# A mask product in bfloat16 instead of float32 in a hybrid decoder block

## The chip, the cores and the metric

The kernel runs on one core of a Trainium2 chip. The metric is the time of one execution on the device in microseconds (us); lower is better. The core has four engines that matter here: TensorE (PE in the profile) multiplies matrices, VectorE (DVE) and ScalarE (ACT) work on elements, GpSimd (POOL) issues the gathers of expert rows. SyncE (SP) issues most of the other transfers. TensorE's weight loads have a row of their own, PEld.

## The reference, cut to what matters

One decoder layer over 1024 tokens of width 1024. Three mixers run on the same normalised input and are merged by gates; an expert layer follows, in which every token takes 16 of 16,384 experts in each of 8 heads. The change touches the first mixer, stick-breaking attention with 8 heads of 64:

```python
def block(args):
    q_blk, n = args
    z = jnp.einsum('bhqd,bhkd->bhqk', q_blk, k).astype(jnp.float32) * scale
    qpos = n * Q_BLOCK + jnp.arange(Q_BLOCK)
    past = kpos[None, :] < qpos[:, None]
    log_keep = jnp.where(past, jax.nn.log_sigmoid(-z), 0.0)
    between = lax.cumsum(log_keep, axis=3, reverse=True) - log_keep
    a = jnp.where(past, jnp.exp(jax.nn.log_sigmoid(z) + between), 0.0)
    return jnp.einsum('bhqk,bhkd->bhqd', a.astype(v.dtype), v)
```

A query sees only keys before its own position. Blocks of 128 keys wholly in the past need no mask; a block on the diagonal does.

## The kernel before, in words

**Tiles and groups.** The 1024 tokens are eight tiles of 128, taken in three groups of 2, 3 and 3 tiles (`GROUPS`). Each group goes through `phase1`: normalisation, projections, stick attention, dilated attention, attention to the memory tokens, gating, output projection and the choice of experts. Tiles 4 and 6 (`DENSE`) later go through all experts in `dense`; the other six fetch their chosen expert rows.

**Stick attention.** `stick_breaking` (line 419) works on four pairs of heads, and in each pair on sub-groups of two tiles (`stick_part`, line 499) or one (`stick_single`, line 450). For every block of 128 keys, from the diagonal back, the scores of both heads go into one PSUM bank `z`. In a diagonal block a second product adds the mask to the scores: the identity `ident` as one operand, the table `diagneg` as the other, -1e30 where a key isn't in the past (lines 463 and 513). ScalarE then takes Abs, Exp and Ln, VectorE forms `sp`, and later products with `ntri` (line 151) add the sums over keys to the same bank before the last Exp. A helper, `Pipe`, issues the second and third part of a block one and two pieces later, so that TensorE has other products in between. A group of 2 tiles has 2 diagonal tiles, a group of 3 has 3; with four pairs and two heads there are 8 tiles x 4 x 2 = 64 mask products. The tables are made once, near the start, on VectorE (lines 147 to 151).

**Products.** Nearly all products go through `mm` (line 112), which issues one and adds its estimated time to a ledger, `cost[0]`. Its rule for a product of n columns and 128 rows is `4 * (n / 2.4 + 2.5)`; a transpose books 120 (`flip`, line 120).

**Expert steps.** `Experts.step` (line 1133) handles four tokens at a time for one of four positions: POOL gathers 128 rows of `u` and 128 rows of `v` (line 1097), 4 KB each; VectorE multiplies and sums (line 1151); after four steps ScalarE takes Gelu, VectorE spreads the weights, and TensorE adds up the rows of `v` (line 1177, eight products a step as the profile counts them). The token's own row is spread over partitions by bfloat16 products with the table `which` (line 1090). There are 768 steps.

**The order.** The program is written out in one order for each engine. A planner at the end of the kernel (lines 1409 to 1446) mixes expert steps with pieces of `phase1` and `dense`. It keeps two clocks. A piece adds its booked cost times `SLOW` (1.38 in phase 1, 1.1 in the dense stage) to `pe`, and its loaded bytes over `BW` (295, then 360) to `dma`. A step adds `TOKEN_NS` = 700 to `pe` and `TOKEN_BYTES` over `BW` to `dma`:

```python
due = max(due + LEAST, pe - LEAST)
while filler[0] is not None and (dma > pe or pe < due):
    a, b = fill(1)
    pe += a
    dma += b
pe += TOKEN_NS
dma += TOKEN_BYTES / bw[0]
if ex.step():
    done += 1
```

So before each step the planner issues mixer or dense pieces until the TensorE clock has reached the DMA clock. When the pieces are used up, the remaining steps run alone. Before the first group has chosen its experts there are no steps to mix in.

Of the kernel before, what the change touches and what calls it, by code (L numbers as in the profile page):

```python
# [7 lines left out]
F32 = mybir.dt.float32  # L8
BF = mybir.dt.bfloat16
# [3 lines left out]
OP = mybir.AluOpType  # L13
# [64 lines left out]
def block_kernel(ctx: ExitStack, tc: tile.TileContext, io):  # L78
    nc = tc.nc
# [16 lines left out]
    const = pool("const", 1)  # L96
# [8 lines left out]
    cost = [0.0]  # L105
# [3 lines left out]
    def bank():  # L109
        return ps.tile([128, 512], F32, name="bank")  # L110

    def mm(out, lhsT, rhs, **kw):
        n = 1
        for d in rhs.shape[1:]:
            n *= d
        cost[0] += 4 * (n / 2.4 + 2.5) * out.shape[0] / 128
        nc.tensor.matmul(out, lhsT, rhs, **kw)  # L117
# [5 lines left out]
    def actf(out, in_, f, **kw):  # L123
        s = SETS.get(f)
        if s and table[0] != s:
            nc.scalar.preload_act_table_set(s)  # L126
            table[0] = s
        nc.scalar.activation(out, in_, f, **kw)  # L128
# [4 lines left out]
    dmat = tmp.tile([128, 2, NS], F32, name="S", bufs=1)[:, 0, :128]  # L133
# [11 lines left out]
    nc.vector.tensor_scalar(dmat, dmat, rows[:, 2:3], None, op0=OP.subtract)  # L145
    ident = keep.tile([128, 128], F32, bufs=1)
    nc.vector.tensor_scalar(ident, dmat, 0.0, None, op0=OP.is_equal)
    diagneg = const.tile([128, 128], F32)
    nc.vector.tensor_scalar(diagneg, dmat, 0.0, -HUGE, op0=OP.is_le, op1=OP.mult)
    ntri = const.tile([128, 128], F32)  # L150
    nc.vector.tensor_scalar(ntri, dmat, 0.0, -1.0, op0=OP.is_le, op1=OP.mult)
# [267 lines left out]
    def stick_breaking(pipe, weights, hT, n0, G, oT):  # L419
        N = G * 128  # L420
        t0 = n0 * 128
        for p in range(4):
# [23 lines left out]
            for i, g in subs(G):  # L446
                args = pipe, kT, v, q[:, :, i * 128:(i + g) * 128], n0 + i, oT[:, p, i * 128:(i + g) * 128]
                yield from stick_single(*args) if g == 1 else stick_part(*args[:5], g, args[5])

    def stick_single(pipe, kT, v, q, n, out):  # L450

        S = tmp.tile([128, 2, NS], F32, name="S", bufs=1)[:, :, :128]
        box = {}
        for b in range(n, -1, -2):
            bs = [b, b - 1][:b + 1]
            m = len(bs)
            z = bank().rearrange("p (x s n) -> p x s n", x=2, s=2)
            for x, y in enumerate(bs):
                for s in range(2):
                    mm(z[:, x, s], kT[:, y * 128:(y + 1) * 128], q[:, s], start=x == 0 and s == 0, stop=False,  # L460
                       skip_group_check=True)
                    if y == n:
                        mm(z[:, x, s], ident, diagneg, start=False, stop=False, skip_group_check=True)
            e = tmp.tile([128, EW], F32, name="e")[:, :512].rearrange("p (x s n) -> p x s n", x=2, s=2)
            actf(e[:, :m], z[:, :m], AF.Abs)
            actf(e[:, :m], e[:, :m], AF.Exp, scale=-1.0)
            actf(e[:, :m], e[:, :m], AF.Ln, bias=1.0)
            sp = tmp.tile([128, 2, NS], F32, name="sp").rearrange("p x (s n) -> p x s n", s=2)
            nc.vector.scalar_tensor_tensor(sp[:, :m], z[:, :m], 0.0, e[:, :m], op0=OP.max, op1=OP.add)

            def part1(b=b, m=m, z=z, e=e, sp=sp):
                for x in range(m):
                    mm(z[:, x], ntri, sp[:, x], start=False, stop=False, skip_group_check=True)
                    if b < n:
                        mm(z[:, x], nones, S, start=False, stop=False, skip_group_check=True)
                if m == 2:
                    mm(z[:, 1], nones, sp[:, 0], start=False, stop=True, skip_group_check=True)
                actf(e[:, :m], z[:, :m], AF.Exp)
                if b >= 2:
                    if b == n:  # L480
                        nc.vector.tensor_add(S, sp[:, 0], sp[:, 1])
                    else:
                        for x in range(m):
                            nc.vector.tensor_add(S, S, sp[:, x])

            def part2(b=b, bs=bs, e=e):
                if b == n:
                    box["o"] = bank()
                for x, y in enumerate(bs):
                    for s in range(2):  # L490
                        mm(box["o"][64 * s:64 * s + 64, :128], v[:, y, 64 * s:64 * s + 64], e[:, x, s],
                           start=y == n, stop=y == 0, skip_group_check=True)
                if bs[-1] == 0:
                    nc.vector.tensor_copy(out, box["o"][:, :128])
            pipe.tick()
            pipe.push(part1, part2)
            yield

    def stick_part(pipe, kT, v, q, n0, G, out):
        N = G * 128  # L500
        nl = n0 + G - 1
        S = tmp.tile([128, 2, NS], F32, name="S", bufs=1)
        box = {}
        for b in range(nl, -1, -1):
            dg = b >= n0
            c0 = (b - n0) * 128 if dg else 0
            off = c0 + 128 if dg else 0
            z = bank().rearrange("p (s n) -> p s n", s=2)
            for s in range(2):
                mm(z[:, s, c0:N], kT[:, b * 128:(b + 1) * 128], q[:, s, c0:N],  # L510
                   start=s == 0, stop=False, skip_group_check=True)
                if dg:
                    mm(z[:, s, c0:c0 + 128], ident, diagneg, start=False, stop=False,
                       skip_group_check=True)
            e = tmp.tile([128, EW], F32, name="e")[:, :2 * NS].rearrange("p (s n) -> p s n", s=2)
            actf(e[:, :, c0:N], z[:, :, c0:N], AF.Abs)
            actf(e[:, :, c0:N], e[:, :, c0:N], AF.Exp, scale=-1.0)
            actf(e[:, :, c0:N], e[:, :, c0:N], AF.Ln, bias=1.0)
            sp = tmp.tile([128, 2, NS], F32, name="sp")
            nc.vector.scalar_tensor_tensor(sp[:, :, c0:N], z[:, :, c0:N], 0.0, e[:, :, c0:N],  # L520
                                           op0=OP.max, op1=OP.add)

            def part1(b=b, c0=c0, off=off, dg=dg, z=z, e=e, sp=sp):
                for s in range(2):
                    mm(z[:, s, c0:N], ntri, sp[:, s, c0:N], start=False, stop=False,
                       skip_group_check=True)
                    if off < N:
                        mm(z[:, s, off:N], nones, S[:, s, off:N], start=False, stop=s == 1,
                           skip_group_check=True)
                actf(e[:, :, c0:N], z[:, :, c0:N], AF.Exp)  # L530
                if b:
                    if dg:
                        nc.vector.tensor_copy(S[:, :, c0:off], sp[:, :, c0:off])
                    if off < N:
                        nc.vector.tensor_add(S[:, :, off:N], S[:, :, off:N], sp[:, :, off:N])

            def part2(b=b, c0=c0, e=e):
                if b == nl:
                    box["o"] = bank()
                for s in range(2):  # L540
                    mm(box["o"][64 * s:64 * s + 64, c0:N], v[:, b, 64 * s:64 * s + 64],
                       e[:, s, c0:N], start=b == nl, stop=b == 0, skip_group_check=True)
                if b == 0:
                    nc.vector.tensor_copy(out, box["o"][:, :N])
            pipe.tick()
            pipe.push(part1, part2)
            yield
# [949 lines left out]
```

## Time and profile before

| | |
|---|---|
| median of 3 runs | 3574.66 us (3574.15 to 3581.68) |
| profiled execution | 3564.13 us, span 3562.4 us |
| mean granted TensorE clock | 0.936 |
| TensorE busy | 3189.3 us, 90% |
| GpSimd busy (gathers) | 1768.1 us, 50% |
| bytes moved by DMA | 1185.56 MB, 333 GB/s |
| of these, gathered expert rows | 805.40 MB |

The profile is one execution; its time lies below the three timed runs. A busy TensorE is not TensorE at its peak, since the length of a product in the profile contains its latency and products overlap. The distance between the starts of two products tells what each takes.

### The profile page before, as it was taken

Reading aid. Unit: us, or ns where it says so; the run is one execution under the profiler, and the core shown is the slowest. Engines: PE = TensorE matmul, PEld = TensorE weight load, DVE = VectorE, ACT = ScalarE, POOL = GpSimd, SP = SyncE. Lnnn points to the kernel's source line nnn. Section 1 sums busy time; section 2 is a strip of 40 time slices with the busy share of each in tenths; the row PEclk is TensorE's granted clock in tenths of the full one; section 3 lists DMA queues with packets and bytes.
Section 4 is the critical chain, followed back from the end, with each engine's and each line's share of the span. In section 5 each row is a group of like instructions: output and inputs, shape, how many; then the busy total and the mean of one; then the engine's idle time right before and its main releaser. Section 6 shows DMA issues by size and latency. Waiting matters only on the chain.

```text
span 3562.4 us, 61070 instructions
## 1 busy us (share of the span) xinstructions
PE 3189.3 (90%) x22930; PEld 2359.5 (66%) x22930; DVE 2356.0 (66%) x6003; ACT 1371.6 (39%) x2747; POOL 1768.1 (50%) x1544
## 2 busy tenths in 40 slices
PE   6999879989999889999998999776779999999954
PEld 6889856656555766666565657654558888888720
DVE  5444597565644469995656665788867677777654
ACT  4443345554411214656544221322224444444410
POOL 0000036655566565766555655566645444544476
PEclk9989989999999999999999999887899999999965
DMA  4425659999899999989998999998999999999999
GB/s 151 140 84 182 221 210 342 336 342 340 318 405 392 403 361 348 331 329 356 328 351 292 391 386 401 350 326 338 399 384 391 365 382 382 390 383 373 349 380 377
DMA packets 346431, 1185.56 MB, mean 333 GB/s; under 512 B 38744, under 2 KB 80216, under 8 KB 326680
## 3 DMA queue, kind: packets, MB, share of 16 engines
q0 software_dynamic: 221184, 805.40, 59.6%
q1 hardware_dynamic: 102672, 337.95, 25.9%
q10 hardware_dynamic: 22280, 38.31, 2.8%
q8 instruction: 181, 2.97, 0.3%
q14 instruction: 114, 0.93, 0.1%
HBM read 1142.18 MB, written 39.32 MB: 332 GB/s over the span
## 4 chain that ended last, share of the span: by engine, by line
PE 60%; DVE 14%; DMA 14%; issue 5%; ACT 4%; POOL 2%; ACTq 0%; SPq 0%; POOLq 0%; DVEq 0%
PE bank L117 30%; PE bank L1195 21%; DMA u<-in_u,iT 7%; PE po L1177 7%; DVE u L1151 4%; DMA v<-in_v,iT 2%; PE pb L1090 2%; DMA b3d<-sp 1%; PE bank L121 1%; POOL u L1097 1%; POOL v L1097 1%; ACT L126 1%; DMA g<-gd 1%; ACT e L128 1%; DMA gd<-g 1%
## 5 line engine op out<-in xcount | busy, mean ns | idle before, releaser
L1097 POOL DMA_INDIRECT u<-in_u,iT x768 | 920.9, 1199 | 965.0 <-DVE i L865 487.7
L1097 POOL DMA_INDIRECT v<-in_v,iT x768 | 846.4, 1102 | 817.8 <-PE po L1177 644.5
L1151 DVE SCALAR_TENSOR_TENSOR u<-u,hb 128x1024 f32<-128x1024 f32 x768 | 927.0, 1223 | 437.6 <-ACT hb L128 274.3
L1177 PE MATMUL po<-v,wz 128*32 128x256 f32 x6144 | 443.7, 416 | 150.2 <-DMA v<-in_v,iT 83.2
L117 PE MATMUL bank<-wide,w 128*128 128x384 f32 x1536 | 520.8, 493 | 2.6 <-DMA w<-in_w_gate 2.6
L117 PEld LDWEIGHTS bank<-wide,w 128*128 128x128 f32 x1536 | 293.1, 193 | 202.7 <-issue 11.2
L1177 PEld LDWEIGHTS po<-v,wz 128*32 128x32 f32 x6144 | 181.8, 115 | 369.6 <-DMA v<-in_v,iT 115.7
L128 ACT ACTIVATE hb<-pb 128x512 f32<-128x512 f32 x384 | 208.2, 595 | 400.0 <-PE pb L1090 257.3
L117 PEld LDWEIGHTS bank<-w,wide 128*128 128x128 f32 x2304 | 263.0, 192 | 7.5 <-issue 2.3
L117 PE MATMUL bank<-w,wide 128*128 128x128 f32 x2304 | 265.3, 275 | 0.2 <-DMA w<-in_w_out 0.2
L1195 PE MATMUL bank<-hh,ul 128*128 128x256 f32 x848 | 240.0, 283 | 1.3 <-DVE ul L1275 1.3
L1195 PE MATMUL bank<-hh,uh 128*128 128x256 f32 x848 | 240.9, 284 | 0.0
L1195 PE MATMUL bank<-hl,uh 128*128 128x256 f32 x848 | 239.9, 283 | 0.0
L128 ACT ACTIVATE e<-bank 128x512 f32<-128x512 f32 (+2 forms) x208 | 109.6, 527 | 277.4 <-PE bank L117 249.3
L1195 PE MATMUL bank<-vh,wh 128*128 128x512 f32 x512 | 203.0, 403 | 2.2 <-ACT vh L128 2.2
L1195 PE MATMUL bank<-vl,wh 128*128 128x512 f32 x512 | 201.8, 394 | 2.4 <-DVE vl L1275 2.3
L1195 PE MATMUL bank<-vh,wl 128*128 128x512 f32 x512 | 199.5, 390 | 0.0
L126 ACT ACT_TABLE_LOAD x144 | 184.8, 1283 | 20.6 <-issue 8.4
L128 ACT ACTIVATE w<-bank 128x256 f32<-128x256 f32 x128 | 49.3, 385 | 366.0 <-PE bank L1195 285.1
L1275 DVE TENSOR_TENSOR vl<-vr,vh 128x1024 fp32r<-128x1024 f32 x128 | 157.1, 1227 | 31.8 <-ACT vh L128 31.8
L117 PE MATMUL bank<-big,w 128*128 128x128 f32 (+1 forms) x1024 | 175.9, 330 | 0.6 <-DMA w<-in_w_pq 0.6
L1195 PE MATMUL bank<-u 128*128 128x256 f32 x544 | 164.9, 303 | 10.2 <-ACT u L128 10.2
(297 smaller groups left out, 5887.9 us busy)
## 6 DMA issues: line engine op xcount, KB each, us to landing
ur<-in_uT SPq DMA_DIRECT2D x64, 1024.0 KB
vr<-in_vd SPq DMA_DIRECT2D x64, 1024.0 KB
w<-in_w_in SPq DMA_DIRECT2D x102, 512.0 KB
w<-in_w_gate SPq DMA_DIRECT2D x72, 512.0 KB
w<-in_w_pq SPq DMA_DIRECT2D x48, 512.0 KB
g<-gd SPq DMA_DIRECT2D x16, 1024.0 KB
w<-in_w_o SPq DMA_DIRECT2D x48, 256.0 KB
w<-in_w_out SPq DMA_DIRECT2D x24, 512.0 KB
```

Of the source, the lines that this page charges most:

```text
L117: nc.tensor.matmul(out, lhsT, rhs, **kw)
L121: nc.tensor.transpose(out, in_, ident)
L126: nc.scalar.preload_act_table_set(s)
L128: nc.scalar.activation(out, in_, f, **kw)
L1090: nc.tensor.matmul(pb, which[:, jj].rearrange("p q s -> p (q s)"), box["b3"][:, f], start=True, stop=True)
L1097: nc.gpsimd.indirect_dma_start(out=t, out_offset=None, in_=io[kind], in_offset=bass.IndirectOffsetOnAxis(ap=ap, axis=0))
L1151: nc.vector.scalar_tensor_tensor(u, u, 1.0, self.hb, op0=OP.mult, op1=OP.mult, accum_out=self.parts[:, i:i + 1])
L1177: nc.tensor.matmul(po[32 * k:32 * k + 32, h:h + 256], wz[:, i, :], v[:, 256 * k:256 * k + 256], start=jj == 0 and i == 0, stop=jj == QB - ...
L1195: nc.tensor.matmul(out, lhsT, rhs, **kw)
L1275: nc.vector.tensor_sub(lo, r[:, x], hi)
```

## The change

The mask product moves from `mm` into a function of its own. Its operands become bfloat16: a second identity table, `eye`, and `diagneg` in bfloat16. The function books 60 in the ledger where `mm` booked 4 x (128 / 2.4 + 2.5) = 223. Both calling places, in `stick_single` and `stick_part`, use it. The identity table `ident` stays float32 for its other users.

```diff
     nc.vector.tensor_scalar(ident, dmat, 0.0, None, op0=OP.is_equal)
-    diagneg = const.tile([128, 128], F32)
+    eye = const.tile([128, 128], BF)
+    nc.vector.tensor_scalar(eye, dmat, 0.0, None, op0=OP.is_equal)
+    diagneg = const.tile([128, 128], BF)
     nc.vector.tensor_scalar(diagneg, dmat, 0.0, -HUGE, op0=OP.is_le, op1=OP.mult)
...
+    def mask(z):
+
+        cost[0] += 60
+        nc.tensor.matmul(z, eye, diagneg, start=False, stop=False, skip_group_check=True)
+
     def stick_single(pipe, kT, v, q, n, out):
...
                     if y == n:
-                        mm(z[:, x, s], ident, diagneg, start=False, stop=False, skip_group_check=True)
+                        mask(z[:, x, s])
...
                 if dg:
-                    mm(z[:, s, c0:c0 + 128], ident, diagneg, start=False, stop=False,
-                       skip_group_check=True)
+                    mask(z[:, s, c0:c0 + 128])
```

## The prediction

> **What bounds the kernel now.** I read the page first, for the balance of the engines and the chain that ended last.
>
> ```profile
> span 3562.4 us, 61070 instructions
> ...
> PE 3189.3 (90%) x22930; PEld 2359.5 (66%) x22930; DVE 2356.0 (66%) x6003; ACT 1371.6 (39%) x2747; POOL 1768.1 (50%) x1544
> ...
> DMA  4425659999899999989998999998999999999999
> ...
> PE bank L117 30%; PE bank L1195 21%; DMA u<-in_u,iT 7%; PE po L1177 7%; DVE u L1151 4%; DMA v<-in_v,iT 2%; PE pb L1090 2%; DMA b3d<-sp 1%; PE bank L121 1%; POOL u L1097 1%; POOL v L1097 1%; ACT L126 1%; DMA g<-gd 1%; ACT e L128 1%; DMA gd<-g 1%
> ```
>
> TensorE is busy for 90% of the span and the chain of waits runs mostly through its products, but from the seventh slice on the DMA engines are also nearly full. So I cut the span into stages: start, stick attention of the first group, rest of that group, the first long stretch in which expert steps run between the pieces of the mixer, the second one, the dense experts, and the end, where only expert steps are left. Columns: time, busy time and instruction count of each engine, granted clock, DMA share, GB/s.
>
> ```profile
> 77.00:134.00 57.00, 57.00 (x456) 53.27 (x455) 19.26 (x29) 26.81 (x49) 0.00 (x0) 1.00 0.50 158
> 134.00:488.00 354.00, 314.89 (x2510) 289.19 (x2510) 200.88 (x540) 139.11 (x294) 0.00 (x0) 0.92 0.47 149
> 488.00:1590.00 1102.00, 1025.60 (x7248) 693.74 (x7247) 740.63 (x2124) 454.65 (x860) 674.39 (x602) 0.97 0.95 355
> 1590.00:2443.00 853.00, 757.56 (x5500) 517.30 (x5498) 568.80 (x1579) 300.73 (x686) 494.70 (x442) 0.93 0.93 348
> ...
> 2650.00:3400.00 750.00, 744.10 (x5316) 630.75 (x5316) 534.91 (x829) 346.12 (x574) 359.53 (x277) 1.00 0.98 376
> 3400.00:3562.00 162.00, 77.53 (x542) 16.04 (x540) 82.06 (x156) 17.66 (x46) 116.06 (x115) 0.55 0.99 389
> ```
>
> The first gather of the expert steps is where I set the third border:
>
> ```profile
> L1097 POOL DMA_INDIRECT u<-in_u,iT x768: 932/940/3240, 488.3 to 3544.1; - x192
> ```
>
> Until 488 us TensorE alone is the limit (57.00 of 57.00 us busy in the first stick stage, DMA half idle). From 488 to 3400 us TensorE and DMA are both near full. In the last 162 us DMA is at 0.99 while TensorE is half idle. Each expert step has two gathers on POOL, so 115 of them are 57.5 steps, or 162 / 57.5 = 2.82 us a step.
>
> Next, the products that change: count, duration and place.
>
> ```profile
> L117 PEld LDWEIGHTS bank<-diagneg,ident x128: 187/192/192, 79.9 to 1642.1; 128*128 128x128 f32 x128
> L117 PE MATMUL bank<-diagneg,ident x128: 271/275/275, 80.0 to 1642.2; 128*128 128x128 f32 x128
> L149 DVE TENSOR_SCALAR diagneg<-S x1: 217/217/217, 6.0 to 6.0; 128x128 f32<-128x128 f32 x1
> ```
>
> ```profile
> 77.00:134.00 57.00, 6.17 (x32) 5.47 (x32) 0.00 (x0) 1.00 0.50 158
> ...
> 488.00:1590.00 1102.00, 16.20 (x84) 13.89 (x84) 0.00 (x0) 0.97 0.95 355
> 1590.00:2443.00 853.00, 2.31 (x12) 1.97 (x12) 0.00 (x0) 0.93 0.93 348
> ```
>
> A float32 product appears as two instructions, so 128 are 64 mask products: 16 in the first group, 48 in the other two, all before 1643 us. Their 275 ns is a latency; what one takes from TensorE is the distance between starts, which the timeline of the first stick block shows (start, length, instruction):
>
> ```profile
> 80.33 0.30 PEld L117 LDWEIGHTS bank<-diagneg,ident 128*128 128x128 f32 x2
> ...
> 80.44 0.39 PE L117 MATMUL bank<-diagneg,ident 128*128 128x128 f32 x2
> ...
> 80.55 0.30 PEld L117 LDWEIGHTS bank<-qpad,big 128*128 128x128 f32 x2
> 80.66 0.60 PE L117 MATMUL bank<-qpad,big 128*128 128x256 f32 x2
> ```
>
> The mask starts at 80.44 and the product behind it at 80.66: 0.22 us for a mask, 0.11 for each half. A weight load starts when the product ahead of it starts, not earlier (the load at 80.55 goes with the mask's second half, which began 0.11 after 80.44), and its own product follows 0.11 later.
>
> **The change part by part.** *The product.* The bfloat16 mask is one instruction with one load, where the float32 mask is two and two. No row shows a 128x128 bfloat16 product; the nearest are the row-spreading products and the loads of other widths:
>
> ```profile
> L1090 PEld LDWEIGHTS <-which x384: 95/98/207, 459.3 to 3522.4; 96*128 96x128 bf16 x192
> L1090 PE MATMUL pb<-b,which x384: 376/381/634, 459.4 to 3522.8; 96*128 96x512 bf16 x192
> ```
>
> ```profile
> 506.53 0.60 PE L1090 MATMUL pb<-b,which 96*128 96x512 bf16 x2
> ```
>
> ```profile
> L117 PEld LDWEIGHTS bank<-ident,s x160: 106/113/158, 485.8 to 2408.4; 128*32 128x32 f32 x160
> ...
> L117 PEld LDWEIGHTS bank<-e,big x416: 132/136/232, 85.4 to 1674.5; 128*64 128x64 f32 x139
> ```
>
> Two bfloat16 products of 512 columns take 0.60 us with 0.38 for the last, so 0.22 between starts; a quarter of the columns is 0.055. That is the lower bound of a mask's price. The bfloat16 load is short (98 ns against 192), so the mask's own weights are ready in time. But float32 loads grow with the columns (113, 136, 192 ns for 32, 64, 128), and the load behind the mask is nearly always a float32 one of 128 columns, which can start only with the mask's product and takes its 0.11: the next product starts 0.11 after the mask, however short that was. This is the upper bound, and my value, since the four lines of the timeline show exactly this succession. Saved per mask: 0.11 us (at most 0.165). The Trainium skill ("TensorE: Matmul & The Clock Gate", Back-to-back issue gap) gives 55.6 ns for a lone 128-column bfloat16 product and about 81 ns in a stream of load and product pairs. With these the sum below would be about -3.7 and -2.7 us. No run here shows either.
>
> *First group, 77 to 134 us.* TensorE has no gap there, and the chain of waits runs through it without a break:
>
> ```profile
> 112.64 2.03 PE bank L1195 x17
> 114.68 1.87 PE bank L117 x12
> 116.55 2.87 PE bank L1195 x24
> 119.42 6.55 PE bank L117 x52
> ```
>
> So 16 x 0.11 = 1.8 us go off the path (at most 16 x 0.165 = 2.6), and all behind starts earlier by as much.
>
> *The ledger.* The diff also replaces the charge that the order planner books for a mask. A product of 128 columns costs 4 x (128/2.4 + 2.5) = 223 in `mm`; `mask` books 60. Times SLOW = 1.38 that is 225 ns less per mask, and 48 x 0.225 = 10.8 us less over groups two and three (in the first no expert step is being balanced). The planner runs mixer pieces until its TensorE clock has caught up with its DMA clock. A step adds TOKEN_BYTES / 295 = 1,073,152 / 295 = 3638 ns to one and 700 to the other, a gap of 2938 ns; with 10.8 us less booked, 10.8 / 2.94 = 3.7 fewer steps stand between the mixer pieces, and 3.7 more are left at the end. Moved with each step are two gathers on POOL's queue, the multiply on DVE, its eight products and a share of the row spreading. Dense pieces keep their own ratio of steps.
>
> *Stretch from 488 us.* If TensorE is the limit there, it gets shorter by 48 x 0.11 = 5.3 us and by the moved steps' products:
>
> ```profile
> 1317.60 3.64 PE po L1177 x32
> ```
>
> Eight of these are 3.64 / 32 x 8 = 0.91 us a step, and half a spreading product is 0.11: 3.7 x 1.02 = 3.8, together 9.1 us (7.9 + 3.8 = 11.7 with the cheaper mask). If DMA is the limit, 3.7 x 1.073 MB at the 355 GB/s of the stage = 11.2 us, and the cheaper mask adds nothing. TensorE at 93% and DMA at 0.95 do not decide it; I take the middle of 9.1 and 11.2, 10.1.
>
> *The end.* 3.7 more steps at 2.82 us: +10.4 us. The chain there is gathers, so nothing hides them:
>
> ```profile
> 3428.50 8.46 DMA u<-in_u,iT
> 3436.98 1.25 DVE u L1151 x2
> 3439.32 7.88 DMA u<-in_u,iT
> ```
>
> *The tables.* `eye` is one more DVE instruction near 6 us, about 0.2 us like the one quoted for `diagneg`. The first product waits for this:
>
> ```profile
> 11.93 0.72 ACT L128 ACTIVATE sq<-big 128x256 f32<-128x256 f32 x2 [9.47 <-DMA big<-in_memT]
> ```
>
> The load of the memory tokens hides it; without that cover it would cost its 0.2 us. Storage is unchanged (two tables of 256 bytes a partition for one of 512).
>
> **Sum.** -1.8 - 10.1 + 10.4 = -1.5 us, with ends -2.6 - 11.7 + 10.4 = -3.9 and -1.8 - 9.1 + 10.4 = -0.5. The profiled execution itself took 3564.13 us (span 3562.4 and 1.7 around it), so it would take 3562.6. It lies 10.5 under the median of the runs, 3574.66, which moves to 3573.2. About 0.2%, 7 us, is what a measurement can tell from no change: I forecast none that can be told.
>
> **Rivals.**
>
> *Faster: the new order closes gaps.* From 488 to 1590 us TensorE is idle 76 us and DMA 5%, 55 us, because steps and mixer pieces wait for each other. ScalarE is among the causes: it swaps its function table whenever a step's Gelu falls between Exp and Ln of an attention block.
>
> ```profile
> 488.00:1590.00 1102.00, 115.47 (x90) 0.97 0.95 355
> ```
>
> 90 swaps of 1.28 us (rows of line 126 alone). Fewer steps there mean fewer swaps: 3.7 steps are about one group of four, at most two swaps, 2.6 us; the rest would have to come from a better fit of the order, a tenth of the gaps, 5 to 8 us. Time: 1.5 + 2.6 + 5 to 8 = 9 to 12 us less, 3562 to 3566. For it: both gaps are real, and a mask stands ahead of the first Abs of its block. Against: such a fit comes by luck, and 48 masks touch only the stick pieces.
>
> *Slower: the stick pieces wait for ScalarE, not TensorE.* Then neither the cheaper mask nor the steps taken out of them shorten the stretch, and the end still grows. The chain inside a stick block of the second group speaks for it:
>
> ```profile
> 569.99 0.60 ACT e L128
> 570.61 1.10 ACT L126
> ...
> 572.61 1.28 ACT L126
> ...
> 575.74 2.59 PE bank L117 x12
> ```
>
> Price: -1.8 + 10.4 = +8.6, 3583. It decides as slower (over 7 us) from the point where the stretches from 488 to 2443 us shrink by less than 1.5 us. Against: the DMA share there is 0.95, and steps taken out do free DMA time.
>
> *The change does not do what it says.* The bfloat16 mask still takes 0.22 us, and only the ledger acts: no first-group gain, 3.8 to 11.2 us off the stretch, +10.4 at the end, -1 to +7: 3574 to 3581, no difference that can be told.
>
> **Chances.** Forecast 0.47, faster rival 0.31, slower rival 0.17, the change without effect 0.05. Faster by over 0.2% is the first rival, 0.31, and 0.02 of the forecast's tail, 0.33; slower 0.17; the same is the other 0.50. The likeliest case alone spans 3570 to 3576 by its terms. The whole range reaches from 3559 (the faster rival with a little more of the gaps) to 3584 (the slower one).
>
> **What would show it.** The mask's rows: 64 instructions instead of 128, type bf16, the next product 0.11 us behind it (0.055 would show the lower bound, 0.22 no gain). The first stick stage shorter by 1.8 us, so the first gather at 486.5 instead of 488.3. In the windows, POOL's count before the dense stage lower by 7 or 8, and the end, after the last dense product, longer by 10 us with 122 or 123 gathers. The forecast is wrong if the end grows while the stretches before do not shrink, if they shrink by much more than 11 us, or if the count of steps at the end stays: then the ledger did not act as I booked it.

## The result

The changed kernel takes 3599.23 us (median of six runs, 3594.38 to 3602.61) against 3575.76 (six runs) before: a ratio of 1.0072, with an interval of 1.0062 to 1.0082. The medians are 23.5 us apart, where 1.5 less was forecast, and the new one lies above the range.

The first lines of the profile after look like those before: the same engines, a little less work, a longer span.

```profile
span 3597.8 us, 60937 instructions
...
PE 3193.8 (89%) x22866; PEld 2359.1 (66%) x22866; DVE 2352.7 (65%) x6004; ACT 1363.4 (38%) x2741; POOL 1760.9 (49%) x1544
...
DMA  4435659889899998999888999998999999999899
...
L1103 POOL DMA_INDIRECT v<-in_v,iT x768 | 850.6, 1108 | 853.2 <-PE po L1183 689.6
L126 ACT ACT_TABLE_LOAD x138 | 177.1, 1283 | 20.7 <-DMA row<-xres 6.0
```

ScalarE swaps its table 138 times, six fewer than before (144), and its busy time fell from 1371.6 to 1363.4 us. The row of the v gathers (busy, mean ns, then idle time ahead of them and who ended it) stood like this before:

```profile
L1097 POOL DMA_INDIRECT v<-in_v,iT x768 | 846.4, 1102 | 817.8 <-PE po L1177 644.5
```

So GpSimd waits 45 us more for the products `po`, which have a line number higher by six now. The mask's rows, by tile, show the product that the diff asked for, and the timeline (start, length) what stands behind it:

```profile
L455 PE MATMUL bank<-diagneg,eye x64: 219/219/314, 80.0 to 1660.1; 128*128 128x128 bf16 x64
```

```profile
80.05 0.22 PE L455 MATMUL bank<-diagneg,eye 128*128 128x128 bf16 x1
80.05 0.30 PEld L117 LDWEIGHTS bank<-qpad,big 128*128 128x128 f32 x2
80.10 0.44 PE L117 MATMUL bank<-qpad,big 128*128 128x128 f32 x2
...
80.38 0.22 PE L455 MATMUL bank<-diagneg,eye 128*128 128x128 bf16 x1
```

64 instructions instead of 128. The record starts the float32 pair 0.05 behind the mask, but that isn't the mask's price: from one mask to the next are 0.33 us, and the pair of 128 columns between them takes 0.22, as the float32 mask did before. So 0.11 are left for the mask. The stages show where the time went. First the windows of the changed kernel, borders at the first gather, the first and the last dense product (columns as before: time, busy time and count of PE, PEld, DVE, ACT, POOL, then granted clock, DMA share, GB/s):

```profile
77.00:134.00 57.00, 57.00 (x452) 52.00 (x451) 20.10 (x31) 26.77 (x51) 0.00 (x0) 1.00 0.51 159
134.00:488.00 354.00, 312.31 (x2498) 287.36 (x2497) 199.31 (x536) 138.72 (x293) 0.00 (x0) 0.93 0.47 149
488.00:2674.00 2186.00, 1946.32 (x13713) 1326.59 (x13712) 1466.70 (x4240) 803.38 (x1723) 1275.05 (x1138) 0.94 0.94 350
2674.00:3424.00 750.00, 744.04 (x5315) 631.73 (x5315) 531.17 (x820) 346.77 (x575) 359.96 (x277) 1.00 0.97 374
3424.00:3597.00 173.00, 84.19 (x578) 17.16 (x576) 87.70 (x167) 18.09 (x46) 125.03 (x123) 0.54 0.99 389
```

The same stretch of the kernel before, as one window:

```profile
488.00:2650.00 2162.00, 1945.53 (x13795) 1325.82 (x13793) 1471.29 (x4241) 812.23 (x1732) 1291.66 (x1146) 0.95 0.95 356
```

Of the profile's 35 us, 11 are at the end (173 against 162) and 24 in the mixer stretch (2186 against 2162). The dense stage is equal. In the stretch eight gathers are gone, which is four steps, and about as many bytes: 350 x 2186 = 765.1 MB against 356 x 2162 = 769.7, or 4.6 MB less. TensorE's busy time is the same to 1 us, though 82 instructions are gone. What grew is idle time, of TensorE by 23 us and of the transfers too.

The profile of the kernel before (3564.13 us) lies 12 us under its median; so 24 may be too much by as much, and medians decide below.

### The profile page after: what moved, and what is told of

It is laid out like the page before. It is cut to its first block, busy times and chain, and to the rows that moved or that the text cites. A ratio compares the mean times of both kernels' runs of the same rounds, so it can differ in the third digit from the quotient of the medians.

```text
span 3597.8 us, 60937 instructions
## 1 busy us (share of the span) xinstructions
PE 3193.8 (89%) x22866; PEld 2359.1 (66%) x22866; DVE 2352.7 (65%) x6004; ACT 1363.4 (38%) x2741; POOL 1760.9 (49%) x1544
## 4 chain that ended last, share of the span: by engine, by line
PE 62%; DVE 15%; DMA 13%; issue 4%; ACT 3%; POOL 2%; ACTq 0%; POOLq 0%; SPq 0%; DVEq 0%
PE bank L117 32%; PE bank L1201 20%; PE po L1183 7%; DMA u<-in_u,iT 6%; DVE u L1157 4%; DMA v<-in_v,iT 2%; DMA b3d<-sp 2%; PE pb L1096 1%; DMA ur<-in_uT 1%; PE bank L121 1%; POOL v L1103 1%; POOL u L1103 1%; DMA gd<-g 1%; DVE v L281 1%; ACT e L128 1%
## 5 line engine op out<-in xcount | busy, mean ns | idle before, releaser
L1103 POOL DMA_INDIRECT u<-in_u,iT x768 | 909.4, 1184 | 971.9 <-DVE i L871 492.2
L117 PEld LDWEIGHTS bank<-big,w 128*128 128x128 f32 x1024 | 161.7, 194 | 18.8 <-issue 1.8
```

The source lines that it names most:

```text
L1103: nc.gpsimd.indirect_dma_start(out=t, out_offset=None, in_=io[kind], in_offset=bass.IndirectOffsetOnAxis(ap=ap, axis=0))
```

## Experiments

Runs come in four sets, each with its own runs of the kernel before on the same chip. The first set's chip ran that kernel in 3572.99 us, the other three in 3744 to 3748 us. So ratios are compared, each against the kernel before on its chip, and nothing is read from absolute times across sets. Diffs are against the changed kernel.

**Which part acts: the product or the ledger.** The first run takes the bfloat16 product with the old charge, the second the float32 product with the new charge.

```diff
 # bfloat16 product, old charge
-        cost[0] += 60
+        cost[0] += 4 * (128 / 2.4 + 2.5)
```

> The bfloat16 product stays, but the planner books for it what it booked for the float32 product (223 instead of 60), so that the program order of ScalarE is that of the kernel before, and the other engines' orders nearly so. Theory A (the loss of the changed kernel, about 24 us, comes from the new order alone): time at the kernel before or up to 7 us below it, 3569 to 3577 us, ratio 0.998 to 1.000; in the stretch up to the first dense product nothing is lost. Theory B (the bfloat16 product itself costs time, by its weight load or by switching between types): most of the 24 us remain, 3590 to 3600 us, ratio above 1.004.

```diff
 # float32 product, new charge
-    eye = const.tile([128, 128], BF)
-    nc.vector.tensor_scalar(eye, dmat, 0.0, None, op0=OP.is_equal)
-    diagneg = const.tile([128, 128], BF)
+    diagneg = const.tile([128, 128], F32)
...
-        nc.tensor.matmul(z, eye, diagneg, start=False, stop=False, skip_group_check=True)
+        nc.tensor.matmul(z, ident, diagneg, start=False, stop=False, skip_group_check=True)
```

> The float32 product of the kernel before, booked at 60 instead of 223: only the order changes, and ScalarE's program order is that of the changed kernel. Theory A (order alone): as slow as the changed kernel or some 2 to 7 us slower, 3597 to 3606 us, ratio 1.006 to 1.009. Theory B (the product): at the kernel before within 5 us, ratio 0.999 to 1.001.

Measured: 3568.75 us, 0.9984 (0.9973 to 0.9994), and 3603.03 us, 1.0087 (1.0074 to 1.0100). The ledger alone makes the kernel slower, without any bfloat16. The product alone gains 0.16%, about 6 us, where the forecast's two terms for it (1.8 and 5.3) make 7; by the two kernels with the new charge, 1.0072 and 1.0087, it is worth about as much.

**How the loss depends on the charge.** If the loss followed from the steps moved, half the change in the charge should give half of it, and a higher charge a gain or nothing.

```diff
-        cost[0] += 60
+        cost[0] += 142        # and in a second kernel 305
```

> The bfloat16 product, booked half way, at 142. Theory A1 (each step that is put off costs time, in proportion): half of the loss, 3583 to 3590 us, ratio 1.002 to 1.004. Theory A2 (the loss belongs to one particular interleaving and does not grow with the booking): any value between about 3565 and 3600 us, not tied to the middle; the end is about 5 us longer than in the kernel before either way.

> The bfloat16 product, booked above the float32 one, at 305 (82 more). Theory A1 (proportion): two steps are moved ahead, the end gets about 5 us shorter and the whole some 10 us faster than the kernel before, 3560 to 3567 us, ratio 0.996 to 0.998. Theory A2 (one particular interleaving): the end gets about 5 us shorter, the stretch before it changes by an amount that the booking does not tell, and the whole can come out on either side of the kernel before.

Measured: 1.0052 (1.0039 to 1.0066) at 142 and 1.0028 (1.0015 to 1.0040) at 305. Both are slower than at 223, though 305 leaves fewer gathers to the end (111 behind the last dense product, against 114). So the sign isn't that of the charge: a change to either side costs.

**Which masks carry the loss.** The charge of 60 for the 24 masks of the second group alone, then for those of the third alone, 223 for the rest.

```diff
+    masks = [0]
...
-        cost[0] += 60
+        masks[0] += 1
+        cost[0] += 60 if 16 <= masks[0] - 1 < 40 else 4 * (128 / 2.4 + 2.5)   # second: masks[0] - 1 >= 40
```

> The bfloat16 product, booked at 60 only in the second group (24 masks, between 488 and 700 us) and at 223 in the others: half of the shift, and all of it early. Theory A1 (a step that is put off costs the same wherever it comes from): half of the loss, 3580 to 3586 us, as the booking of 60 in the third group alone. Theory A2 (a step's cost depends on the piece it stands between, and the loss comes where the steps leave the stretch from 1130 to 1640 us, in which they cost nothing): nearly the whole loss, 3588 to 3600 us, since that stretch already sees the shift.

> The bfloat16 product, booked at 60 only in the third group (24 masks, from 1280 us on). Theory A1: half of the loss, 3580 to 3586 us, as with the second group alone. Theory A2: the order up to about 1280 us is that of the kernel before, so the loss between 1130 and 1300 us is gone and what is left is the end, four steps or about 11 us longer, less what they free earlier: 3568 to 3582 us, clearly below the second group alone.

Measured: second group 1.0063 (1.0043 to 1.0082), two thirds of the changed kernel's loss on such a chip (1.0092, below); third group 0.9986 (0.9965 to 1.0008), none, though both leave 119 gathers to the end, five more than with the old charge. With the third group the stretch gave back what the end took, as the forecast had it for all three. The same number of moved steps costs most of the loss in one place and nothing in another.

**The same shift without the masks.** Old charges throughout, and the 10.8 us of the ledger taken off in one piece, just ahead of the dense stage.

```diff
-        cost[0] += 60
+        cost[0] += 4 * (128 / 2.4 + 2.5)
...
+        cost[0] -= 10800 / 1.1        # ahead of the dense stage
```

> The bfloat16 product booked at 223 everywhere, so that the order up to the dense stage is that of the kernel before; once, where the dense stage begins, 10.8 us are taken from the planner's TensorE clock, so that about four steps move from there to the end. It measures the end's price alone: if a step costs in the dense stage what it costs at the end (DMA is the limit of both), no change against the booking of 223, 3565 to 3573 us; if it costs only its TensorE time of about 1 us in the dense stage and 2.8 us at the end, 7 us more, 3573 to 3580 us; if it costs nothing in the dense stage, 11 us more, 3577 to 3584 us.

Measured: 1.0024 (1.0000 to 1.0047) with 124 gathers at the end instead of 114. At 2.82 us for two gathers ten are 14 us at the end, of which some 9 remain. The interval reaches from 0 to 18. Moving steps to the end costs a part of the loss at most; the rest of it hangs on where the steps were missing before.

**A small nudge.** The charge lowered by 33 only.

```diff
-        cost[0] += 60
+        cost[0] += 190
```

> The bfloat16 product, booked at 190, 33 less than the float32 one was: 2.2 us less over 48 masks, less than one step. Theory A1 (proportion): a fifth of the loss, 5 us above the booking of 223, 3572 to 3577 us. Theory A2 (the particular interleaving): the order changes in places all the same, and the time can be anything from 3560 to 3600 us; a value more than 10 us away from 3569 speaks for A2.

Measured: 1.0128 (1.0094 to 1.0162), the slowest of all charges, with 116 gathers at the end. Ahead of the dense stage stand 1146, as with the old charge: on balance no step has left the mixer stretch. A fifth of the change in the charge costs more than the whole. This ends every account by which the loss is a price for each step that is moved.

**The shift at two other places.** Old charges, the 10.8 us taken off once ahead of the second group's stick attention, and in the other kernel once ahead of its choice of experts.

```diff
-        cost[0] += 60
+        cost[0] += 4 * (128 / 2.4 + 2.5)
...
+        if gidx == 1:
+            cost[0] -= 10800 / 1.38
```

> The bfloat16 product booked at 223 everywhere, and once, before the stick attention of the second group, 10.8 us taken from the planner's TensorE clock: the whole shift at one place, no mask booked differently. From the end of that stage on, TensorE's order is nearly that of the changed kernel (82% of its instructions stand at the same place). Theory A (the order alone): as slow as the changed kernel, ratio 1.005 to 1.009. If the loss hung on the booking or on the masks themselves: as the booking of 223, 0.997 to 1.000.

> The same 10.8 us taken once, before the second group chooses its experts (about 1180 us); up to there the order is that of the kernel before. Theory A2 (a step put off costs where it leaves pieces that do not get shorter without it, in the stretch of the second group before 1180 us and in the choice of experts behind it): the first part of the loss is missing, the second and the end remain: ratio 1.001 to 1.006, below the offset before the stick attention. Theory A1 (every step put off costs alike): the same as the offset before the stick attention, within 0.15%.

Measured: 1.0046 (1.0027 to 1.0065) and 1.0066 (1.0041 to 1.0090). With every mask charged as before, a hole of four steps in the second group costs half to seven tenths of the loss. It isn't the masks or their own moment that matter.

**The buffers of v.** The waits of GpSimd in the stretch, 488 to 2650 us (total, times, longest), for the kernel with the old charge and bfloat16, on the first chip:

```profile
POOL v L1103 <- PE po L1183: 377.6, 179, 11.8
```

and for the changed kernel:

```profile
POOL v L1103 <- PE po L1183: 415.9, 191, 14.4
```

A gather of `v` can't be issued until one of six buffers (`VP`) is free, and a buffer is freed by the `po` products that read it. To see whether this wait sets the pace, both charges were run with five buffers.

```diff
-UP, VP = 5, 6
+UP, VP = 5, 5
...
-        cost[0] += 60                        # old charge: in the first kernel only
+        cost[0] += 4 * (128 / 2.4 + 2.5)
```

> The bfloat16 product booked at 223, with five buffers for the gathered rows of v instead of six; ScalarE's order is unchanged. It tells what POOL's wait for a free v buffer is worth. If that wait sets the pace of the stretches with expert steps, one buffer less costs 1 to 4%, ratio 1.01 to 1.04; if it is covered by other waits, under 0.3%, ratio below 1.002.

> The order of the changed kernel (booking of 60) with five buffers for v. Theory C (the loss of the new order is POOL waiting for v buffers that late products hold): fewer buffers make it worse, and the distance to the booking of 223 with five buffers is more than 1.2%. If the loss lies in other waits (the mixer's own chain, DVE), the distance stays at 0.7 to 1.0%, or shrinks.

Measured: 1.0202 (1.0173 to 1.0231) with the old charge, 1.0194 (1.0166 to 1.0221) with the new one. One buffer less costs 2%, so with five the wait does set the pace. But the expectation that the distance between the charges would widen fell: with five buffers they are equal. That the old order is a good one only for six buffers would explain it, but no run shows that; so this pair shows that five buffers bind, and neither what the sixth still leaves nor that the buffers are the whole of the loss. A seventh buffer, which would be the direct test, wasn't tried.

**The first pair again, and a shift to the other side.** On a chip of the slower kind, the two charges once more, and the old charge with 10.8 us added ahead of the dense stage.

```diff
-        cost[0] += 60                 # old charge: in the first and third kernel
+        cost[0] += 4 * (128 / 2.4 + 2.5)
...
+        cost[0] += 10800 / 1.1        # third kernel only, ahead of the dense stage
```

> The bfloat16 product booked at 223, once more, as the common base of the runs with offsets. If the order is what counts on any chip: ratio 0.997 to 1.000, and the offset towards the end (1.0024) then cost 0.3 to 0.5%.

> The changed kernel itself, once more, beside the booking of 223 on one chip. Theory A (order): ratio 1.005 to 1.009 also here, and 0.7 to 1.0% above the booking of 223. If the loss is tied to the speed of one chip's memory, it is under 0.4% on a slower chip, and the equal times of the two orders with five buffers say nothing about the buffers.

> Booked at 223, and once, where the dense stage begins, 10.8 us added to the planner's TensorE clock, so that up to four steps move from the end towards the dense stage. If the end's steps are the dear ones (2.8 us each against about 1 us of TensorE time in the dense stage), some 3 to 10 us faster than the booking of 223; if DMA is the limit of both, the same within 3 us; if the stretch before the first dense product has no room for them, slower by some 5 to 10 us.

Measured: old charge 1.0000 (0.9984 to 1.0015), changed kernel 1.0092 (1.0074 to 1.0110), so the loss stands on both kinds of chip. The added offset gave 1.0001 (0.9981 to 1.0020) with 111 gathers at the end instead of 114. Fewer steps at the end brought nothing that can be told (three gathers would be 4 us, and the interval is 7 to either side). No order of these is measurably faster than that of the bfloat16 product with the old charge, 0.9984 on one chip and 1.0000 on the other.

**Where the stretch loses it.** Three pairs of windows on the first chip, cut between the same mixer pieces, first a short one in which steps are missing. The kernel with the old charge:

```profile
1350.00:1390.00 40.00, 34.02 (x219) 21.41 (x218) 33.22 (x118) 12.75 (x34) 24.16 (x23) 0.91 1.03 402
```

its `po` products alone (PE and PEld):

```profile
1350.00:1390.00 40.00, 7.10 (x96) 2.69 (x96) 0.91 1.03 402
```

the changed kernel:

```profile
1361.39:1404.18 42.79, 33.68 (x187) 21.80 (x186) 35.25 (x114) 12.76 (x34) 24.14 (x20) 0.84 0.92 362
```

and its `po` products:

```profile
1361.39:1404.18 42.79, 4.30 (x64) 1.91 (x64) 0.84 0.92 362
```

96 products are twelve steps, 64 are eight, and the 32 are the only instructions that TensorE has fewer (187 against 219). Four steps fewer saved nothing: the piece took 2.8 us longer. By TensorE's account they were worth 4.1 (1.02 each), by the transfers' 12.1 (11.2 / 3.7 each). At one place the piece's own chain is seen to set the time. In the changed kernel TensorE stands idle for VectorE:

```profile
1396.25 10.00 PE L117 MATMUL bank<-wide,w 128*128 128x384 f32 x22 [6.63 <-DVE wide L341]
```

With the old charge the `po` products of four steps stand in the gap ahead of the same product (1374.83 to 1383.27 us). That such a chain sets the whole piece is an inference.

A long piece, from the second group's choice of experts into the third group, first with the old charge:

```profile
1141.00:1610.00 469.00, 431.19 (x3270) 319.48 (x3266) 365.52 (x1177) 194.04 (x371) 283.69 (x254) 0.96 0.96 361
```

then in the changed kernel:

```profile
1142.00:1633.00 491.00, 438.70 (x3262) 323.02 (x3261) 364.59 (x1172) 194.28 (x369) 288.02 (x253) 0.94 0.93 344
```

The `po` products in these windows are 1032 and 1024, so 129 and 128 steps. As many steps to one, the same bytes (361 x 469 = 169.3 MB, 344 x 491 = 168.9), 22 us more. Of these, 14.5 are idle time of TensorE (37.8 and 52.3 us). The rest is busy time, 7.5 us more for eight products fewer, and the granted clock is 0.94 instead of 0.96. Not all 22 us stay: the first dense product comes 15.6 us later, at 2674.0 instead of 2658.4. How a moved step makes engines wait is seen inside the piece. Timelines of the changed kernel (in brackets the idle time ahead and its releaser), VectorE:

```profile
1237.88 0.29 DVE L1172 TENSOR_TENSOR wz<-gel,spread 128x128 f32<-128x128 f32 x1
```

TensorE:

```profile
1235.30 11.86 PE L117 MATMUL bank<-big,w 128*128 128x256 f32 x64
1246.99 0.83 PE L117 MATMUL bank<-big,e 128*128 128x128 f32 x6
1247.76 1.93 PE L1183 MATMUL po<-v,wz 128*32 128x256 f32 x32
```

GpSimd:

```profile
1233.37 0.93 POOL L1103 DMA_INDIRECT u<-in_u,iT  x1 [0.30 <-issue]
1248.70 0.94 POOL L1103 DMA_INDIRECT v<-in_v,iT  x1 [14.40 <-PE po L1183]
```

The weights `wz` of four steps are ready at 1238.17, but their 32 products stand on TensorE's queue behind 64 products of a projection and 6 more, and start 9.6 us later. Until then no buffer of `v` is free, GpSimd stands for 14.40 us, and behind it stand the gathers of `u` as well, since they share its queue. With the old charge the same products are ahead of the projection. VectorE:

```profile
1227.85 0.28 DVE L1172 TENSOR_TENSOR wz<-gel,spread 128x128 f32<-128x128 f32 x1
```

TensorE:

```profile
1228.18 2.39 PE L1183 MATMUL po<-v,wz 128*32 128x256 f32 x32
1231.06 1.06 PE L121 MATMUL bank<-ident,wide 128*128 128x128 f32 x8 [0.48 <-DVE wide L833]
1231.96 10.64 PE L117 MATMUL bank<-big,w 128*128 128x256 f32 x64
```

GpSimd:

```profile
1229.57 0.94 POOL L1103 DMA_INDIRECT v<-in_v,iT  x1 [4.97 <-PE po L1183]
```

There GpSimd waits 4.97 us. The charge had moved the four steps to the other side of one projection. The same 64 products take 11.86 us instead of 10.64, at a granted clock of 0.90 instead of 1.00. But this long wait isn't lost time one for one: six `bank<-big,e` products that start at 1286.46 us with the old charge start at 1286.82 in the changed kernel, so some 40 us later the mixer is 0.4 us late, with four steps fewer done.

The loss shows behind that place, in the third pair of windows. Old charge:

```profile
1286.40:1389.90 103.50, 93.67 (x665) 71.27 (x664) 73.33 (x265) 26.90 (x79) 62.01 (x58) 0.95 1.02 401
```

Changed kernel, from the same product to the same product:

```profile
1286.80:1404.10 117.30, 96.86 (x666) 73.65 (x665) 83.44 (x282) 27.78 (x80) 66.98 (x60) 0.91 0.96 365
```

Each holds 224 `po` products, 28 steps. It takes 13.8 us more, of which TensorE's idle time is 10.6 (9.8 and 20.4 us). TensorE's wait for the weights `wz` makes most of that, first with the old charge, then in the changed kernel (total, times, longest):

```profile
PE po L1183 <- DVE wz L1172: 3.8, 3, 2.2
PE po L1183 <- DVE wz L1172: 13.6, 4, 5.7
```

So a moved step can also stand too early. In the changed kernel the `po` products come ahead of the next 32 products of a projection, and TensorE stands until the weights are there:

```profile
1303.49 0.83 PE L117 MATMUL bank<-big,e 128*128 128x128 f32 x6
1310.02 3.30 PE L1183 MATMUL po<-v,wz 128*32 128x256 f32 x32 [5.69 <-DVE wz L1172]
1313.70 5.40 PE L117 MATMUL bank<-big,w 128*128 128x256 f32 x32
```

With the old charge those 32 stand ahead of the next `po` products, and the wait is 2.20 us:

```profile
1302.39 5.40 PE L117 MATMUL bank<-big,w 128*128 128x256 f32 x32
1307.63 0.83 PE L117 MATMUL bank<-big,e 128*128 128x128 f32 x6
1310.66 3.28 PE L1183 MATMUL po<-v,wz 128*32 128x256 f32 x32 [2.20 <-DVE wz L1172]
```

**Over all runs.** GpSimd's wait for `po` in the window 488 to 2650 us of each profile follows the time roughly within each kind of chip. First chip: 374.2 us (before) and 377.6 (0.9984), 377.2 (305, 1.0028), 403.8 (float32 at 60, 1.0087), 413.4 (142, 1.0052), 415.9 (changed, 1.0072). The others: 364.3 (third group, 0.9986), 367.4 (added offset, 1.0001), 392.8 (old charge, 1.0000), 400.7 (offset ahead of stick, 1.0046), 403.2 (second group, 1.0063), 414.3 (ahead of dense, 1.0024), 423.5 (ahead of the choice, 1.0066), 442.1 (changed, 1.0092), 474.3 (190, 1.0128), 488.0 and 496.6 (five buffers, 1.0194 and 1.0202). The row with the largest sum of six buffers is that of the charge 190 (the longest single wait, 27.3 us, is that of the charge 142):

```profile
POOL v L1103 <- PE po L1183: 474.3, 117, 23.8
```

It isn't a strict order (305 has no longer wait and is slower, 142 waits longer than float32 at 60 and is quicker, and ahead of dense a part lies at the end), and one profile of each kernel stands beside a median. On the slower chips the window ends ahead of the first dense product, which comes at 2793 to 2861 us. And GpSimd's busy time is nearly the same in all, so a longer span must show as its idle time somewhere: the sum says where it stands, not that this is the cause. The other wait belongs beside it, TensorE's for `wz` in the same window: 54.1 us before, 56.1 with the old charge, 70.5 in the changed kernel. No strict order either: the third group alone has 76.8 us and loses nothing. But it fits the charge 305, whose loss GpSimd's wait doesn't show:

```profile
PE po L1183 <- DVE wz L1172: 84.3, 32, 13.2
```

## Why the prediction was wrong

The step that failed is the term "Stretch from 488 us", -10.1: there the stretch was held to be limited by TensorE or by the transfers, and only the choice between 9.1 and 11.2 was left open. It grew instead, by 18 us against the old charge with the same product (whose profiled run lay 9 us above its median, so 18 is rather too little) and by 24 against the profile before. Of the 18, some 11 are idle time of TensorE and 7 are busy time, with 34 instructions fewer. By the prediction's steps:

*The mask's price* was right: 64 products, 0.11 us each. The Trainium skill ("TensorE: Matmul & The Clock Gate", Back-to-back issue gap) has about 81 ns for a product in a stream of load and product pairs; the trace does not bear that out here, where a float32 load stands behind it and the rows give 0.11.

*The first group, -1.8.* The last `bank<-S,none` products of that stage did start 1.8 us earlier, at 128.34 instead of 130.12 us, but the first gather came at 488.7 instead of 486.5 (488.3 before):

```profile
L1103 POOL DMA_INDIRECT u<-in_u,iT x768: 932/940/2012, 488.7 to 3579.2; - x192
```

Behind the stick attention TensorE waits for ScalarE. Before:

```profile
166.38 0.70 PE L117 MATMUL bank<-sq,ones 128*128 128x256 f32 x2 [0.58 <-ACT sq L128]
```

and after:

```profile
165.63 0.70 PE L117 MATMUL bank<-sq,ones 128*128 128x256 f32 x2 [1.62 <-ACT sq L128]
```

Of 1.8 us, 0.75 are left here, and none can be told by 488, since the first gather lies anywhere from 488.0 to 494.8 us in the profiles. That the path runs through TensorE without a break was shown for the first stick stage and used up to 488.

*The ledger* was right: 1138 gathers instead of 1146 before the dense stage, four steps for 3.7. (That nearly all products go through `mm` is too much said: 10,352 of TensorE's 22,930 instructions do by their line. The masks are among them, so their 223 stands.) *The end* was right: +11 in the profile for +10.4, with 123 gathers in the window for 122 or 123.

*The stretch.* Two things were wrong in it. Steps taken out of mixer pieces were credited with their share of TensorE or transfers, and where four were missing nothing came back (40.0 to 42.8). And the steps that stayed were taken to run as before, while the order around them moved too: in the long piece as many steps took 22 us more. That a share of 0.95 and a busy time of 93% mean a full resource was the wrong reading. The waits of GpSimd for `po`, 644.5 of its 817.8 idle us ahead of v gathers, stood in the page before and were not read: they say that the transfers start by leave of TensorE's queue, and so by the order. In the same order TensorE itself stood longer for weights of steps that came too early (56.1 to 70.5 us).

*The rivals.* The slower one had the right sign and the right condition, a stretch that doesn't shrink, but its price of +8.6 was the end alone and its cause, ScalarE, has no part in it that any run shows: ScalarE has less work, and the wait of TensorE that grew most is one for VectorE's `wz`. Its 3583 is 16 us short. The faster one counted on fewer table swaps; six fewer came, 7.7 us of ScalarE, and the time grew. No rival let a different order make the gaps larger, though the faster one let it close them. The one without effect of the product had the ledger alone act, which is most of what happened, but its -1 to +7 us gave the stretch the same credit.

*What stays open.* The end's 10 us are shown. Of the stretch it is shown that the order alone, with any product, makes the loss, mostly from the second group; that one buffer of `v` less costs 2%; and, in a piece that takes 13.8 us more, that most of it is TensorE's idle time in the new order. That such waits make up the whole 18 us isn't shown, nor what lowers the granted clock where TensorE stands more.

## What to carry to other kernels

Before crediting a saving in a stage where two resources look full, read who holds the gathers back: a share of 0.95 and 93% here hid waits in which the buffers of one engine hang on the queue of another, and the order, not the work, made the difference. A charge in a planner's ledger is a change of the program's order; when the work of an instruction changes, try the new instruction with the old charge first, since here no other order was measurably quicker. And price a reordering to both sides, for a nudge of a fifth can cost more than the whole.

## What was not expected of the hardware

The time is very sensitive to the order: a charge of 190 instead of 223 for the masks, with the same instructions, takes 1.28% more than the kernel before. And chips differ: the same kernel takes 3573 us on one and 3744 to 3748 on three others. With the old charge, the dense stage is equal (754 us on the first chip, 756 on the last), and the difference lies in the stages with more gathers. Beside the mixers, on the last chip:

```profile
488.00:2828.00 2340.00, 2009.10 (x13752) 1355.74 (x13747) 1469.87 (x4245) 814.20 (x1731) 1274.34 (x1145) 0.92 0.89 329
```

On the first, the same program:

```profile
490.00:2658.00 2168.00, 1939.77 (x13747) 1321.35 (x13746) 1472.18 (x4242) 811.54 (x1731) 1285.72 (x1146) 0.94 0.94 355
```

As many products and gathers take 172 us more, at 329 instead of 355 GB/s and a transfer share of 0.89 instead of 0.94. The end, where only expert steps are left, is 16 us longer too. On the last chip, then on the first:

```profile
3585.00:3764.00 179.00, 82.45 (x542) 17.39 (x540) 82.06 (x156) 18.00 (x46) 123.36 (x115) 0.53 0.93 352
3412.00:3575.00 163.00, 80.27 (x544) 16.66 (x543) 82.49 (x157) 17.97 (x46) 116.85 (x115) 0.53 0.98 387
```

So it isn't the mixers beside the gathers that make the chip slower. What does is open.
